# The recurrence of a hybrid transformer step: full-row tiles at two levels, moved transposes and increments, another mixer entry

## The chip, the cores and the metric

The kernel runs on one core of one Trainium2 chip. The metric is device time in microseconds (us). The kernel before was timed three times: median 2933.15 us, from 2932.75 to 2934.38. The engines are named as in the profile: PE is the matrix engine (PEld its weight loads), DVE the vector engine, ACT the scalar engine, POOL the general one, SP the queue that issues most DMAs.

## The reference, cut to what matters

One layer of a diffusion backbone on 1024 latent and 128 context tokens, width 1024: half a feed-forward block, a token mixer, the other half feed-forward block, each behind a normalisation with shift and scale. The mixer adds attention and a recurrence that runs forward and backward, and the recurrence is what the change is about.

```python
h = rmsnorm(x, g) * (1 + scale) + shift                  # the mixer's entry
q = silu(hq); v = hi; f = lb + (1 - lb) * sigmoid(hf)    # 8 heads of 64 keys, 64 values
# for each head and direction, token by token; k_t = 1 - f_t
S_t = diag(f_t) S_{t-1} + k_t outer v_t
o_t = S_t^T q_t
o_rec = rmsnorm(o_fw + flip(o_bw), hg_norm_g) * silu(hgate)
```

## The kernel before

Tokens lie along the free axis, 1152 columns (1024 latent, 128 context) in three chunks of 384. `ORDER` is (2, 0, 1), the order in which chunks are taken. Every large product is done in three single-pass parts of split numbers (`mm3`: high times high, high times low, low times high), which is why each weight and each activation exists as a high part (`wh`, `xh`) and a low part (`wl`, `xl`).

**The mixer's entry.** The first feed-forward block ends in `down_last`, which goes chunk by chunk and normalises a finished chunk (`norm`, lines 381 to 406) while the next is computed. The norm of the last chunk is left over as a generator, `self.tail`; the mixer advances it while it projects the other two chunks. `norm` first calls `stat_end`: one matmul `nps` with a matrix of ones sums the squares, then Ln and Exp on ACT and three DVE steps make the factor `rs`. For each of 8 row blocks it then multiplies on DVE, scales and shifts on ACT, rounds to `xh` on ACT and takes the rest `xl` on POOL.

**The recurrence** is `hgrn`. A head's forward direction lies in partitions 0 to 63 (`A`), its backward direction in 64 to 127 (`B`). For a chunk, `scan_pre` makes decayed keys `Kb`, `KE` and queries `Qb`, `QP` for blocks of 8 tokens. `scan_lev` then builds the token-by-token matrix `Af` by doubling: a base step (`Kb` with `Qb`, masked on DVE into the tiles `A`), then levels m = 8, 16, 32 and 64. At each level PE multiplies key copies `kr[m]` with `QP` into a PSUM tile `lv`; then DVE (rows B) and POOL (rows A) decay half of `QP`, which may start when the level's matmuls have read it and must end before the next level's; DVE decays `KE`, and ACT copies the next level's keys from it (`key_half`). `kr[m]` holds forward keys in the first half of each pair of blocks and backward keys in the second. At levels 8 and 16 one matmul over all 128 rows does both directions, with zeros in the other halves, and the result is masked. At levels 32 and 64 the directions are apart: rows A and rows B go to two `lv` tiles (lines 892 to 894), which ACT copies to `Af` (lines 913 and 914). There are three `lv` tiles (PSUM banks), taken in turn. After level 64, `kt` transposes `KE` through PE, ACT copies it to `kT`, and `dS` multiplies it with the values: the chunk's increment of the state. `scan_out` (after the third chunk) runs the state chain `S` on DVE and multiplies out (`po`).

**The order.** All of this is woven by generators: at each `yield` of `scan_lev` the loop in `hgrn` (lines 778 to 780) lets 12 large matmuls of a projection run (`mm`, half of one `dense_g` tile), and one step of the next chunk's `scan_pre`. So a chunk is: base, 12 mm, level 8, 12, level 16, 12, level 32, 12, level 64, 12, `kt`, 12, `dS`, 12. A scheduler then fixes each engine's order from this text; an engine runs its instructions in that order and waits where an operand is late. In every second head from the third on, the projections begin with `proj_gate`, which normalises the previous pair's output (`rec_norm`: matmuls `ops`, Ln and Exp with table loads on ACT, steps on DVE).

Of the kernel before, what the change touches and what calls it, by code (L numbers as in the profile page):

```python
# [19 lines left out]
P = 128  # L20
# [68 lines left out]
class Trunk:  # L89
# [3 lines left out]
    def run(self):  # L93
        self.part, self.mode, self.chunks, self.bg = {}, "ffn1", ORDER, iter(())
        nc, tc, a = self.nc, self.tc, self.a
        with ExitStack() as st:
            self.cp = st.enter_context(tc.tile_pool(name="cp", bufs=1))
            self.wp = st.enter_context(tc.tile_pool(name="wp", bufs=1))
            self.tp = st.enter_context(tc.tile_pool(name="tp", bufs=25))
            self.dp = st.enter_context(tc.tile_pool(name="dp", bufs=1, space=DRAM))  # L100
            self.consts()
            self.xs = self.dp.tile([KT, P, T], F32, name="xs")
            self.modt = self.cp.tile([P, 9, KT, 2], F32, name="modt")
            self.gs = self.cp.tile([P, 3, KT, 2], F32, name="gs")
            with ExitStack() as s1:
                self.ffn_pools(s1)
                self.start()
                self.ffn_fast(0, 2, 1)
            self.mode = "mix"
            with tc.tile_pool(name="mp", bufs=1) as mp:  # L110
                self.mixer_consts(mp)
                self.mixer()
            with ExitStack() as s1:
                self.mode = "ffn2"
                self.ffn_pools(s1)
                self.merge()
                self.ffn_fast(1, 8, 3)
# [263 lines left out]
    def norm(self, c, i):  # L381

        nc = self.nc
        lo, hi = span(c)
        cs = slice(lo, hi)
        rs = self.rs[:, cs]
        if self.mode != "mix":
            rs = self.bank("ps1", "rsp", hi - lo)
        self.stat_end(c, rs)
        yield  # L390
        for k in range(KT):
            t = self.fp.tile([P, hi - lo], F32, tag=self.nt[0], bufs=self.nt[1], name="xn")
            nc.vector.tensor_mul(t, self.x[k][:, cs], rs)
# [11 lines left out]
            nc.gpsimd.tensor_sub(tl, t, th)  # L405
            yield
# [204 lines left out]

    def mixer_consts(self, cp):
        nc, a = self.nc, self.a
# [5 lines left out]
        nc.vector.memset(self.onesb, 0.0)  # L619
# [34 lines left out]
    def proj_f(self, i, h, out):  # L654
        nc = self.nc
        fs = out["f"] = self.tt(F32, "fs")
        nc.vector.memset(fs[64:P, 0:1], 1.0)
        w = self.load_w(self.a["w_in"][i], KT, P, home="pieces" if i == 0 else "low")
        for c in ORDER:
# [16 lines left out]
    def proj_v(self, i, out):  # L676
        nc = self.nc
        V = out["V"] = self.tt(F32, "V")
        w = self.load_w(self.a["w_in"][i], KT, P, home="low")
        for c in ORDER:  # L680
# [34 lines left out]
    def hgrn(self):  # L715
        nc = self.nc
        self.mmb = 2
# [7 lines left out]
        self.A2 = f32("A2", [P, 3, G])  # L725
        for t in self.XY:
            nc.vector.memset(t[:, :, 3:4], 1.0)
        for t in self.A1 + [self.A2, self.kr[8], self.kr[16]]:
            nc.vector.memset(t, 0.0)
        self.cnt = 0  # L730
# [34 lines left out]

        d = scan_of(0)
        for _ in self.scan_pre(d, ORDER[0]):
            pass
# [72 lines left out]
    def scan_lev(self, d, b):  # L841
# [20 lines left out]
        def products(parts, k, q, blocks):  # L862
            for j in range(3):
                kj, qj = k[:, ts(j, P)], q[:, ts(j, P)]
                for ki, qi in blocks:
                    for r, ps in parts:
                        ks, qs = (ki, qi) if r != B else (qi, ki)
                        n = qs.stop - qs.start
                        nc.tensor.matmul(ps[ks, j, :n], kj[r, ks], qj[r, qs], start=True, stop=True)

# [15 lines left out]
        for li, m in enumerate((8, 16, 32, 64)):  # L886
            kr = self.kr[m]
            if m < G:
                ps = lv()
                products([(slice(0, P), ps)], kr, qp, diag)  # L890
            else:
                pair = (A, lv()), (B, lv())
                blocks = [(slice(u, u + m), slice(u + m, u + 2 * m)) for u in range(0, P, 2 * m)]
                products(pair, kr, qp, blocks)
            tv = Tm.rearrange("p (n h) -> p n h", h=2)
# [13 lines left out]
            if m < G:  # L909
                nc.vector.copy_predicated(A1, mb(2 + li), ps[:, :, :G])  # L910
            else:
                for u, v in blocks:
                    nc.scalar.copy(Af[u, :, v], pair[0][1][u, :, :m])
                    nc.scalar.copy(Af[v, :, u], pair[1][1][v, :, :m])
            if m == 16:
# [10 lines left out]
        nc.scalar.copy(kT, pt)  # L926
        yield
        pd = self.pp.tile([P, 3, 64], F32, tag="sm", bufs=3, name="dS")
# [4 lines left out]
        nc.scalar.copy(dS[:, 3 * b : 3 * b + 3], pd)  # L933
        yield

# [676 lines left out]
    def ffn_fast(self, l, gm, nxt):  # L1612
# [228 lines left out]
```

## Time and profile before

| What | us |
|---|---|
| median of 3 runs | 2933.15 |
| the profiled execution | 2932.25 |
| its span, first to last instruction | 2930.1 |
| feed-forward 1 with its end | to about 832 |
| recurrence with its projections | about 832 to 1472 |
| attention | to about 1914 |
| output, feed-forward 2, final norm | to the end |

The page of the profile gives for each engine the time in which it was busy. PE is busy nearly all the time everywhere, so what is to be read is the small rest: which instruction PE stood before, what released it, and at which clock PE ran. A row of the timeline reads: start, duration, engine, line, operation, output<-inputs, shape, count, and in brackets how long the engine was idle before it and what ended that. A view of stretches gives busy time of each engine between two times and the granted PE clock (1.00 is full). "mm" rows are the large projection matmuls; one with 384 columns starts about 0.175 us after the one before at full clock, 0.32 us at half.

### The profile page before, as it was taken

How to read it: one execution, taken by the hardware profiler on the slowest of the kernel's cores; microseconds unless marked ns; L12 is line 12 of the kernel's file. 1: busy time of each engine (PE TensorE's matmuls, PEld its weight loads, DVE VectorE, ACT ScalarE, POOL GpSimd, SP SyncE). 2: the span in 40 equal slices, each digit the busy share in tenths (PEclk: the TensorE clock that was granted, in tenths of full speed). 3: DMA queues.
4: the chain of work that ended last, by engine and by line, in shares of the span. 5: the costliest groups of instructions: out<-in, count | busy, mean ns of one | idle time of the engine just before them, and what ended most of it. 6: DMA issues, size and time to landing. Idle time of an engine off the chain costs nothing. (4 is left out here: it accounts for less than half of the span.)

```text
span 2930.1 us, 54396 instructions
## 1 busy us (share of the span) xinstructions
PE 2833.2 (97%) x20946; PEld 2668.0 (91%) x20946; DVE 1976.7 (67%) x4282; ACT 1285.9 (44%) x2574; POOL 957.3 (33%) x904
## 2 busy tenths in 40 slices
PE   6999999999999999999998999999999999999998
PEld 5999999999988888888996877699999999999997
DVE  7677777677678777777357777856665665556665
ACT  6432323321176666666536777721552332232112
POOL 0133322444132122222145444532342222235431
PEclk9999999999999999999998999999999999999999
DMA  6643333643111111111200001242542322235211
GB/s 245 206 146 122 122 127 111 255 162 119 61 61 66 40 55 42 55 42 53 73 31 14 16 18 34 74 163 72 165 147 93 108 83 75 75 120 199 92 46 65
DMA packets 151492, 282.44 MB, mean 96 GB/s; under 512 B 19201, under 2 KB 83777, under 8 KB 151233
## 3 DMA queue, kind: packets, MB, share of 16 engines
q1 hardware_dynamic: 151088, 278.90, 27.8%
q8 instruction: 165, 2.70, 0.4%
q14 instruction: 95, 0.77, 0.1%
q10 hardware_dynamic: 144, 0.07, 0.0%
HBM read 215.37 MB, written 63.52 MB: 95 GB/s over the span
## 5 line engine op out<-in xcount | busy, mean ns | idle before, releaser
L1590 PE MATMUL b<-xo,wo 128*128 128x288 f32 x3552 | 484.6, 296 | 0.0
L1590 PEld LDWEIGHTS b<-xo,wo 128*128 128x128 f32 x3552 | 476.4, 188 | 0.0
L483 DVE SCALAR_TENSOR_TENSOR x<-dn,modt,x 128x256 f32<-128x256 f32 (+4 forms) x728 | 353.3, 505 | 169.0 <-PE dn L456 168.1
L454 PE MATMUL mm<-xh,wh 128*128 128x384 f32 (+1 forms) x1008 | 363.5, 361 | 5.7 <-DVE q L673 3.7
L1590 PE MATMUL b<-bh,wo 128*128 128x288 f32 x1776 | 366.4, 295 | 0.6 <-ACT et L1600 0.6
L456 PE MATMUL mm<-xh,wl 128*128 128x384 f32 (+1 forms) x1008 | 342.8, 340 | 0.3 <-DVE wl L228 0.2
L455 PE MATMUL mm<-xl,wh 128*128 128x384 f32 (+1 forms) x1008 | 342.3, 340 | 0.0
L1590 PEld LDWEIGHTS b<-bh,wo 128*128 128x128 f32 x1776 | 289.2, 188 | 0.9 <-ACT et L1600 0.9
L1590 PE MATMUL b<-bl,wo 128*128 128x288 f32 x888 | 261.9, 295 | 0.0
L243 POOL TENSOR_TENSOR wl<-raw,wh 128x1024 fp32r<-128x1024 f32 (+3 forms) x71 | 152.0, 2142 | 267.8 <-ACT wh L242 265.0
L1565 ACT CAST wo<-raw 128x512 fp32r<-128x512 f32 x185 | 114.7, 621 | 229.5 <-PE b L1590 119.3
L454 PEld LDWEIGHTS mm<-xh,wh 128*128 128x128 f32 (+1 forms) x1008 | 189.8, 188 | 19.6 <-DVE q L673 4.3
L1566 DVE TENSOR_TENSOR wo<-raw,wo 128x512 fp32r<-128x512 f32 x185 | 127.1, 688 | 104.8 <-ACT wo L1565 101.9
L454 PE MATMUL dn<-hh,wh 128*128 128x384 f32 (+2 forms) x576 | 196.2, 341 | 1.3 <-DVE et L1606 0.8
L456 PE MATMUL dn<-hh,wl 128*128 128x384 f32 (+2 forms) x576 | 194.6, 338 | 1.0 <-POOL wl L243 1.0
L455 PE MATMUL dn<-hl,wh 128*128 128x384 f32 (+2 forms) x576 | 194.2, 337 | 0.0
L455 PEld LDWEIGHTS mm<-xl,wh 128*128 128x128 f32 (+1 forms) x1008 | 190.4, 189 | 1.9 <-issue 0.4
L456 PEld LDWEIGHTS mm<-xh,wl 128*128 128x128 f32 (+1 forms) x1008 | 189.9, 188 | 1.8 <-DVE wl L228 0.5
L1668 POOL TENSOR_TENSOR hl<-hr,hh 128x1152 fp32r<-128x1152 f32 x44 | 118.0, 2693 | 194.5 <-ACT hh L1667 100.7
L314 DVE SCALAR_TENSOR_TENSOR junk<-wada,cb 128x512 bf16<-128x512 f32 x224 | 165.0, 737 | 7.1 <-DMA wada<-in_w_aT 6.3
L1322 POOL TENSOR_TENSOR ehl<-e,ehl 128x512 fp32r<-128x512 f32 x93 | 122.6, 1323 | 141.7 <-ACT ehl L1320 78.8
L1590 PEld LDWEIGHTS b<-bl,wo 128*128 128x128 f32 x888 | 167.4, 189 | 0.0
(391 smaller groups left out, 6904.2 us busy)
## 6 DMA issues: line engine op xcount, KB each, us to landing
raw<-in_w SPq DMA_DIRECT2D x148, 256.0 KB, 3.2
raw<-in_w SPq DMA_DIRECT2D x58, 512.0 KB, 3.5
wada<-in_w_aT SPq DMA_DIRECT2D x112, 256.0 KB, 2.9
hr<-hs SPq DMA_DIRECT2D x44, 576.0 KB, 5.2
hs<-et SPq DMA_DIRECT2D x148, 144.0 KB, 1.7
raw<-in_w_in SPq DMA_DIRECT2D x41, 512.0 KB, 3.2
hb<-hd SPq DMA_DIRECT2D x44, 288.0 KB, 3.5
x<-in_xT SPq DMA_DIRECT2D x16, 576.0 KB, 6.4
```

The lines of the kernel that those rows point to most:

```text
L243: pin((eng or self.nc.gpsimd).tensor_sub(wl, raw, wh))
L314: nc.vector.scalar_tensor_tensor(junk, ws[n % 2], 1.0, cs[s], ALU.mult, ALU.mult, accum_out=o)
L454: pin(nc.tensor.matmul(ps, wh, xh, start=start and i == 0, stop=False))
L455: pin(nc.tensor.matmul(ps, wh, xl, start=False, stop=False))
L456: pin(nc.tensor.matmul(ps, wl, xh, start=False, stop=stop and i == n - 1))
L483: nc.vector.scalar_tensor_tensor(self.x[m][:, a:b], ps[:, a - lo : b - lo], self.modt[:, gm, m, s : s + 1], self.x[m][:, a:b], ALU.mult, A ...
L1322: eng.tensor_sub(el, e, eh)
L1565: nc.scalar.copy(wh, src[i])
L1566: nc.vector.tensor_sub(wl, src[i], wh)
L1590: nc.tensor.matmul(ps, w[:, k], x[:, k, :QW], start=first, stop=last, skip_group_check=home != i)
L1668: nc.gpsimd.tensor_sub(hl, raw, hh)
```

## The change

Seven edits, all around the mixer:

1. Levels 32 and 64 use one `lv` tile and matmuls over all 128 rows, as levels 8 and 16 do; the list of block pairs holds each pair in both orders. For this all four `kr` are cleared at the start, not two.
2. The copies to `Af` stand right behind the level's matmuls in the text, ahead of the decay.
3. The `yield` between level 64 and the transposes `kt` is gone; there is a second one behind level 8 and behind `kt`; the one behind `dS` is gone, so `dS` comes just ahead of the next chunk's base.
4. The last chunk's norm in the mixer: scale in the first DVE step, shift and rounding in one ACT step, the low part on DVE. Its `stat_end` has high priority.
5. The constants of the mixer (`mixer_consts`) are made and the mask is loaded during the first feed-forward block, the mask over SP's queue. The pool `mp` is gone.
6. The first chunk's `scan_pre` starts in the middle of the first projections, the clearing of the tiles is pinned behind the norm, and the weights of the projections `q` and `v` of the first pair are split in two pieces.
7. `tp` has 27 tiles of a full row block where it had 25; a scratch area for DMA descriptors is made smaller.

```diff
-            self.tp = st.enter_context(tc.tile_pool(name="tp", bufs=25))
+            self.tp = st.enter_context(tc.tile_pool(name="tp", bufs=27))
...
-            with tc.tile_pool(name="mp", bufs=1) as mp:
-                self.mixer_consts(mp)
-                self.mixer()
+            self.mixer()
...
+        last = self.mode == "mix"
+        if last:
+            with self.tc.high_priority(offset=600):
+                self.stat_end(c, rs)
+        else:
+            self.stat_end(c, rs)
...
+            if last:
+                for a, b, s in segs(c):
...
+                    nc.vector.scalar_tensor_tensor(v, self.x[k][:, a:b], g, rv, ALU.mult, ALU.mult)
+                    nc.scalar.activation(th, v, AF.Identity, bias=sh)
+                    nc.vector.scalar_tensor_tensor(tl, v, sh, th, ALU.add, ALU.subtract)
+                yield
+                continue
...
-        nc.scalar.dma_start(mf, a["mask"])
+        nc.sync.dma_start(mf, a["mask"])
...
-        w = self.load_w(self.a["w_in"][i], KT, P, home="low")
+        w = self.load_w(self.a["w_in"][i], KT, P, home="pieces" if i == 2 else "low")
...
-        for i, _ in enumerate(weave(feed(0))):
-            if i < 12:
-                next(self.tail, None)
-            if i == 11:
-                assert next(self.tail, 1)
...
-        d = scan_of(0)
-        for _ in self.scan_pre(d, ORDER[0]):
+        pre = iter(())
+        for i, _ in enumerate(weave(feed(0))):
+            if i < 12:
+                next(self.tail, None)
+            if i == 11:
+                assert next(self.tail, 1)
+                for t in self.XY:
+                    pin(nc.vector.memset(t[:, :, 3:4], 1.0))
+                d = scan_of(0)
+                pre = self.scan_pre(d, ORDER[0])
+            if i == 13:
+                for t in self.A1 + [self.A2] + list(self.kr.values()):
+                    pin(nc.vector.memset(t, 0.0))
+            next(pre, None)
+        for _ in pre:
             pass
...
-                        ks, qs = (ki, qi) if r != B else (qi, ki)
-                        n = qs.stop - qs.start
-                        nc.tensor.matmul(ps[ks, j, :n], kj[r, ks], qj[r, qs], start=True, stop=True)
+                        n = qi.stop - qi.start
+                        nc.tensor.matmul(ps[ki, j, :n], kj[r, ki], qj[r, qi], start=True, stop=True)
...
-            kr = self.kr[m]
-            if m < G:
-                ps = lv()
-                products([(slice(0, P), ps)], kr, qp, diag)
-            else:
-                pair = (A, lv()), (B, lv())
+            ps = lv()
+            blocks = diag
+            if m >= G:
                 blocks = [(slice(u, u + m), slice(u + m, u + 2 * m)) for u in range(0, P, 2 * m)]
-                products(pair, kr, qp, blocks)
+                blocks = [c for k, q in blocks for c in ((k, q), (q, k))]
+            products([(slice(0, P), ps)], self.kr[m], qp, blocks)
+            if m >= G:
+                for k, q in blocks:
+                    nc.scalar.copy(Af[k, :, q], ps[k, :, :m])
...
-            else:
-                for u, v in blocks:
-                    nc.scalar.copy(Af[u, :, v], pair[0][1][u, :, :m])
-                    nc.scalar.copy(Af[v, :, u], pair[1][1][v, :, :m])
...
             Tm = Tn
-            yield
+            if m < 64:
+                yield
+            if m == 8:
+                yield
...
         nc.scalar.copy(kT, pt)
+        yield
         yield
...
         nc.scalar.copy(dS[:, 3 * b : 3 * b + 3], pd)
-        yield
...
         if l == 0:
+            self.mixer_consts()
```

How the order moves, at three places. **PE, a chunk in the middle of a head** (`lv` are the recurrence's level matmuls, those with `Qb,Kb` the base; the rows left out are the projection matmuls `mm`, 12 in each gap of the first piece). Before:

```order
L869 MATMUL lv<-Qb,Kb 32x32 x24
...
L869 MATMUL lv<-QP,kr_9029 32x32 x12
...
L869 MATMUL lv<-QP,kr_9030 32x32 x12
...
L869 MATMUL lv<-QP,kr_9031 32x32 x12
...
L869 MATMUL lv<-QP,kr_9032 64x64 x6
...
L924 MATMUL kt<-ident,KE 128x128 x3
...
L932 MATMUL dS<-V,kT 64x64 x6
```

Now, with 12 rows of `mm` in each gap but 24 in the gap behind the first level and in the one behind `kt`:

```order
L949 MATMUL dS<-V,kT 64x64 x6
L885 MATMUL lv<-Qb,Kb 32x32 x24
...
L885 MATMUL lv<-QP,kr_9026 32x32 x12
...
L885 MATMUL lv<-QP,kr_9027 32x32 x12
...
L885 MATMUL lv<-QP,kr_9028 32x32 x12
...
L885 MATMUL lv<-QP,kr_9029 64x64 x6
L940 MATMUL kt<-ident,KE 128x128 x3
```

Levels 16, 32 and 64 come 12 `mm` later after the base, `kt` follows level 64 at once, and `dS` stands 24 `mm` behind `kt` and directly ahead of the next base.

**DVE, first chunk of a head that begins with `proj_gate`** (`rt`, `osq` and `oT` are the steps of `rec_norm`, `QP` the decay of the queries: 64x12x16 between levels 16 and 32, 64x6x32 between 32 and 64). Before:

```order
L905 TENSOR_TENSOR QP<-QP,T_11346 64x12x16
L910 COPY_PREDICATED A_0_9035<-mask,lv 128x96
L917 TENSOR_TENSOR Ad<-A_0_9035,A_9037 128x96
L363 SCALAR_TENSOR_TENSOR rt<-ops,osq 128x384 x2
L364 SCALAR_TENSOR_TENSOR rt<-rt,osq 128x384 x2
L365 SCALAR_TENSOR_TENSOR osq<-rt,osq 128x384 x2
L968 SCALAR_TENSOR_TENSOR oT<-oT,vec,osq 128x384 x2
L363 SCALAR_TENSOR_TENSOR rt<-ops,osq 128x384
L905 TENSOR_TENSOR QP<-QP,T_11421 64x6x32
```

Now:

```order
L361 SCALAR_TENSOR_TENSOR rt<-ops,osq 128x384 x2
L362 SCALAR_TENSOR_TENSOR rt<-rt,osq 128x384 x2
L363 SCALAR_TENSOR_TENSOR osq<-rt,osq 128x384 x2
L984 SCALAR_TENSOR_TENSOR oT<-oT,vec,osq 128x384 x2
L361 SCALAR_TENSOR_TENSOR rt<-ops,osq 128x384
L922 TENSOR_TENSOR QP<-QP,T_11327 64x12x16
L362 SCALAR_TENSOR_TENSOR rt<-rt,osq 128x384
L927 COPY_PREDICATED A_0_9032<-mask,lv 128x96
L363 SCALAR_TENSOR_TENSOR osq<-rt,osq 128x384
L930 TENSOR_TENSOR Ad<-A_0_9032,A_9034 128x96
L984 SCALAR_TENSOR_TENSOR oT<-oT,vec,osq 128x384
L715 TENSOR_TENSOR sg<-mm,sg 128x384
```

The decay that level 32 needs stood ahead of `rec_norm` and now stands behind nine of its twelve steps; the one that level 64 needs (64x6x32) is now the row after the last one shown.

**PE, the mixer's entry** (`dn` is the end of the feed-forward block, `nps` the sum of squares for the last chunk). Before, `nps` stands behind the first 12 `mm`:

```order
L456 MATMUL dn<-hh,wl 128x384
L454 MATMUL mm<-xh_8434,wh 128x384
...
L456 MATMUL mm<-xh_8440,wl 128x384
L438 MATMUL nps<-rs,ones 128x384
L454 MATMUL mm<-xh_8434,wh 128x384
```

Now it stands ahead of them:

```order
L467 MATMUL dn<-hh,wh 128x384
L468 MATMUL dn<-hl,wh 128x384
L469 MATMUL dn<-hh,wl 128x384
L451 MATMUL nps<-rs,ones 128x384
L467 MATMUL mm<-xh_8446,wh 128x384
```

What had filled PE while the squares were summed up now comes after the sum.

More of the change, by code (lines that the diff above doesn't have):

```diff
@@ L392, in norm @@
             t = self.fp.tile([P, hi - lo], F32, tag=self.nt[0], bufs=self.nt[1], name="xn")
+            if last:
+                for a, b, s in segs(c):
+                    v, th, tl = t[:, a - lo : b - lo], self.xh[k][:, a:b], self.xl[k][:, a:b]
+                    g, sh = self.gs[:, i, k, s : s + 1], self.modt[:, 3 * i, k, s : s + 1]
+                    rv = rs[:, a - lo : b - lo]
+                    nc.vector.scalar_tensor_tensor(v, self.x[k][:, a:b], g, rv, ALU.mult, ALU.mult)
[3 more added lines that the diff above has]
+                continue
             nc.vector.tensor_mul(t, self.x[k][:, cs], rs)
@@ L657, in proj_f @@
         nc.vector.memset(fs[64:P, 0:1], 1.0)
-        w = self.load_w(self.a["w_in"][i], KT, P, home="pieces" if i == 0 else "low")
+        w = self.load_w(self.a["w_in"][i], KT, P, home="pieces" if h == 0 else "low")
         for c in ORDER:
@@ L678, in proj_v @@
         V = out["V"] = self.tt(F32, "V")
-        w = self.load_w(self.a["w_in"][i], KT, P, home="low")
+        w = self.load_w(self.a["w_in"][i], KT, P, home="pieces" if i == 3 else "low")
         for c in ORDER:
@@ L715, in hgrn @@
     def hgrn(self):
-        nc = self.nc
+        nc, pin = self.nc, self.tc.keep_in_program_order
         self.mmb = 2
@@ L725, in hgrn @@
         self.A2 = f32("A2", [P, 3, G])
[L726 to L729, printed above, removed]
         self.cnt = 0
@@ L1819 @@
     from concourse.bass_utils import run_bass_kernel_spmd
-    nc = _bacc.Bacc("TRN2", target_bir_lowering=False, num_devices=1)
+    nc = _bacc.Bacc("TRN2", target_bir_lowering=False, num_devices=1, dynamic_dma_scratch_size=1024)
     arrays = layout(inputs)
```

5 lines of the change are left out of this document (2 added, 3 removed).

## The prediction

> **What bounds the kernel now.** I read the page first, then a table of stretches of the recurrence, then the waits of PE there, then the timeline at the longest of them.
>
> ```profile
> span 2930.1 us, 54396 instructions
> PE 2833.2 (97%) x20946; PEld 2668.0 (91%) x20946; DVE 1976.7 (67%) x4282; ACT 1285.9 (44%) x2574; POOL 957.3 (33%) x904
> ```
>
> PE is busy for 97% of the span, so a change can win only what PE stands, or runs slowly, in the stage that is changed. The stretches show the recurrence (1028 to 1172 is one period of two heads) and four windows of 3.4 us:
>
> ```profile
> core 0: us, PE busy (x) PEld busy (x) DVE busy (x) ACT busy (x) POOL busy (x), PEclk, DMA share, GB/s
> 832.00:905.00 73.00, 63.60 (x459) 58.13 (x459) 56.38 (x133) 56.15 (x118) 25.99 (x33) 0.95 0.15 51
> 1028.00:1172.00 144.00, 138.01 (x1544) 122.34 (x1543) 108.51 (x276) 96.06 (x225) 31.45 (x52) 0.99 0.14 48
> 1037.10:1040.50 3.40, 1.82 (x14) 1.44 (x13) 2.56 (x6) 3.25 (x11) 1.54 (x2) 1.00 0.16 60
> 1040.50:1043.90 3.40, 3.40 (x14) 3.30 (x13) 2.18 (x4) 2.46 (x5) 1.25 (x1) 0.50 0.00 0
> 1078.10:1081.50 3.40, 1.93 (x20) 1.52 (x18) 2.47 (x10) 3.25 (x12) 0.00 (x0) 1.00 0.02 5
> 1081.50:1084.90 3.40, 3.40 (x22) 3.33 (x21) 2.21 (x4) 3.26 (x9) 1.64 (x4) 1.00 0.07 28
> ```
>
> A period loses 6.0 us to standing. The mixer's entry loses 9.4 of 73. The fourth row is a second loss: after a window in which PE was busy for 1.82 of 3.40 us, the next one ran at clock 0.50. The window at 1078.10 was hardly busier (1.93), and the next one kept clock 1.00. Who holds PE up, from 905 to 1456 us:
>
> ```profile
> PE lv L869 <- ACT Af L913: 10.3, 9, 1.6
> PE dS L932 <- ACT kT L926: 3.1, 3, 1.0
> PE lv L869 <- ACT kr L882: 2.4, 3, 0.8
> PE lv L869 <- DVE QP L905: 1.8, 5, 0.7
> ```
>
> The first row is the bank wait: level 64 takes two `lv` tiles of three and stands until ACT has copied level 32 out of one. The second is `dS`, only 12 `mm` behind the transposes.
>
> **The change part by part.** *One tile per level.* A chunk takes six `lv` tiles instead of eight; level 64 then gets the bank of level 8, which DVE has read long before. Of the nine bank waits three, of 1.58 us, are where a head begins with `proj_gate`; the other six make 10.3 - 3 x 1.58 = 5.6 us. All of it can go, or none if another operand is as late; I take 5.
>
> The three places with `proj_gate` are worked out alone, since the order changes there:
>
> ```profile
> 1037.10 0.53 ACT L362 ACTIVATE osq<-osq 128x384 f32<-128x384 f32 x1
> 1037.35 0.33 PE L454 MATMUL mm<-xh,wh 128*128 128x384 f32 x1
> 1037.66 0.56 DVE L363 SCALAR_TENSOR_TENSOR rt<-ops,osq 128x384 f32<-128x384 f32 x1 [0.34 <-ACT osq L362]
> 1038.25 0.61 DVE L905 TENSOR_TENSOR QP<-QP,T 64x192 f32<-64x192 f32 x1
> 1039.25 0.56 PE L869 MATMUL lv<-QP,kr 64*64 64x64 f32 x6 [1.58 <-ACT Af L913]
> 1040.57 0.52 PE L456 MATMUL mm<-xh,wl 128*128 128x384 f32 x1
> ```
>
> Before, PE reached 1037.35 with levels 16 and 32 done and stood until 1039.25, then ran a window at half clock: 10 or 11 `mm` at 0.32 instead of 0.175 us, 1.5 us lost. Now DVE decays `QP` for level 32 only behind the third `rt`. That step waits for the Exp that ended at 1037.6; the decay would end near 1038.5. PE, with 36 `mm` before it as before, would want level 32 at about 1037.2: a new wait of 1.3 us. Level 64 comes 11 `mm` later (1.9 us), while DVE still has six steps of about 0.5 us ahead of its decay: another 0.5. Per place 1.58 + 1.5 - 1.8 = 1.3, three times 3.9. If PE stands as long as before and the clock drops again, it is -2; if neither wait comes, 9.
>
> What the full rows cost PE stands in one chunk:
>
> ```profile
> 887.85 0.40 PE L869 MATMUL lv<-QP,kr 128*32 128x32 f32 x24
> 893.08 0.39 PE L869 MATMUL lv<-QP,kr 64*32 64x32 f32 x24
> 896.89 0.63 PE L869 MATMUL lv<-QP,kr 64*64 64x64 f32 x12 [1.12 <-POOL QP L905]
> 902.60 0.57 PE L932 MATMUL dS<-V,kT 128*64 128x64 f32 x12 [0.35 <-ACT kT L926]
> ```
>
> The same 24 records take 0.40 us on full rows (level 8) and 0.39 on half rows (level 32); 12 records with 64 columns take 0.57 (`dS`, which also waited before it) and 0.63. I take 0. A full-row matmul must also wait for both halves of `QP`; that is inside the waits above.
>
> *Twice the distance.* `dS` gets 24 `mm` (4.2 us) behind `kt` instead of 2.1; its longest wait is 1.0. The waits go: 3.1 us, and 0.35 in the row just shown: 3.5, between 0 and that. Level 16 gets the same; the rows charge it with 0.65 once, left in the range.
>
> *`dS` joined to the base.* Each change from `mm` to a small group and back costs PE:
>
> ```profile
> 901.91 0.34 PE L456 MATMUL mm<-xh,wl 128*128 128x384 f32 x1
> 903.10 0.44 PE L454 MATMUL mm<-xh,wh 128*128 128x384 f32 x1
> 905.13 0.34 PE L456 MATMUL mm<-xh,wl 128*128 128x384 f32 x1
> 905.40 0.62 PE L869 MATMUL lv<-Qb,Kb 64*32 64x32 f32 x48
> 905.95 0.44 PE L454 MATMUL mm<-xh,wh 128*128 128x384 f32 x1
> 906.23 0.33 PE L455 MATMUL mm<-xl,wh 128*128 128x384 f32 x1
> ```
>
> From 905.13 to 906.23 are 1.10 us, two `mm` steps would be 0.35: the base costs 0.75, of which 0.10 is the entry (0.27 to its start instead of 0.175) and 0.10 the slower first `mm` behind it (0.28); `dS` hands over in about 0.1 more. One such crossing less is about 0.3 us, in two chunks of three of 8 heads: 16 x 0.3 = 4.8, at least 0 and at most 16 x 0.55, the whole of one entry and one exit. Level 64 with `kt` behind it saves nothing sure, since `kt` had no gap before; `KE` for `kt` is decayed one chunk ahead in DVE's order, so I add no wait.
>
> *The state chain.* At a head's end `dS` now lies 12 `mm` nearer to `po`:
>
> ```profile
> 1086.28 0.57 PE L932 MATMUL dS<-V,kT 128*64 128x64 f32 x12
> 1090.04 2.78 DVE L943 SCALAR_TENSOR_TENSOR S<-S,Gall,dS 64x64 f32<-64x64 f32 x9
> 1091.18 0.44 PE L953 MATMUL po<-Af,V 128*64 128x128 f32 x4
> ```
>
> With `dS` 2.1 us later, at 1088.4, a copy on ACT ends it before 1090.04, when DVE comes to the chain anyway; and `po` needs only its first three steps (0.9 us) at once. Cost 0. Without that cover it is up to 1 us at each of 8 heads.
>
> *The entry.*
>
> ```profile
> 836.81 0.91 PE L438 MATMUL nps<-rs,ones 128*128 128x384 f32 x2 [1.59 <-DVE rs L379]
> 842.13 0.17 DVE L619 MEMSET onesb<- 128x128 f32 x1 [2.03 <-POOL xl L405]
> 844.71 0.54 DVE L363 SCALAR_TENSOR_TENSOR rt<-nps,rs 128x384 f32<-128x384 f32 x1
> 853.16 0.69 PE L454 MATMUL mm<-xh,wh 128*128 128x384 f32 x1 [2.48 <-DVE q L673]
> ```
>
> DVE's steps up to `rs` are the same, so `nps` still starts near 836.8, and the 12 `mm` that ran before it are put behind it: 2.1 us lost, PE stands 4.4 instead of 1.59. In return the clearing of the constants (842.13 to 844) and the wait for POOL ahead of it leave DVE, and `rt` can start some 2 us sooner. ACT loses one step for each of 8 blocks, POOL one, DVE gains one of 0.54 us: 4.3 us more work on DVE. Against the 2.48 us at 853.16 I set a like wait, as the first sigmoid now stands on ACT behind three new rounding steps. I take 0, between -6 (the 4.3 and 2.1 uncovered) and +5 (the wait at 853.16 and the 2.1 us by which the norm comes sooner, with that loss hidden). The mask's load, 27 tiles, the earlier constants and the split weights cost nothing where PE does not wait for them; the two pieces cost ACT one more start each.
>
> The waits for `kr` and the other `QP` (4.5 us) I leave as they are. **Sum:** 5 + 3.9 + 3.5 + 4.8 = 17.2 from the profiled execution's 2932.25 (its span and 2.15 around it): 2915.0; the median of the runs is 0.9 above it: 2916, rounded to **2915** for the small gains left out. By its terms' bounds the likeliest case reaches from 2905 to 2925.
>
> **The clock, by the skill.** The row said that 1.58 us of standing were enough for a window at 0.50. The Trainium skill, "TensorE: Matmul & The Clock Gate", section "Why this matters for your kernels", asks only for no gap over some 3 us. By that rule the 1.5 us per `proj_gate` place would not be there to win (the sum would be 4.5 us smaller) and the 4.4 us at the entry would cost a window. The trace contradicts it for the first; the second it cannot show.
>
> **The rivals.** (a) *The wait moves on.* ACT, not the bank, is late: in the window at 1037.10 it is busy for 3.25 of 3.40 us. Then PE meets the same lateness at the next ACT result (`kr`, the sigmoid that frees an `mm` tile), and only the joining stays: 2933.15 - 4.8 = 2928. For it: the waits on `kr` in the list. Against: next to ACT's 96.06 of 144 us over a period there is room, and what level 64 waited for is truly a bank.
>
> (b) *Slower: the two halves ran side by side.* If matmuls on rows A and on rows B overlap, full rows take twice as long at levels 32 and 64: 24 chunks x (0.39 + 0.63) = 24.5 us lost, 2915 + 24.5 = 2940. It decides once a pair of levels takes over 0.7 us more than before. Against it stands the pair 0.40 and 0.39.
> The Trainium skill, "TensorEngine Tiling (Array Packing)", section "Theoretical Speedup", gives up to 2x for a dimension up to 64 by such tiles, which speaks against this change; the trace does not agree, by that pair.
>
> (c) *All waits go* and nothing returns, at the gates and at `kr`: 2915 - 5 - 4.5 = 2905.
>
> **How the numbers follow.** Forecast 0.64, (a) 0.17, (b) 0.08, (c) 0.11. What can be told from no change is 0.2%, 5.9 us, so below 2927.3 is faster: forecast, (c), and a third of (a), 0.80; the rest of (a) with little else, 0.12; (b) 0.08. The range, 2904 to 2931, holds the forecast, (a) and half of (c).
>
> **What would show it.** Right: no wait of `lv` on `Af`, none of `dS` on `kT`; `nps` behind an idle time over 4 us; at the three gates level 32 waits about 1 us for DVE's `QP` and no window at 0.50 follows; level groups of 24 records still near 0.4 us. Wrong: a new long row of PE waits on `QP`, `kr` or `KE`, more windows at half clock, or level 32 at 0.8 us.

## The result and the profile after

| | us |
|---|---|
| kernel before, median of 20 runs | 2932.61 (2929.70 to 2935.93) |
| changed kernel, median of 20 runs | 2926.81 (2922.73 to 2931.57) |
| ratio | 0.998, 95% interval 0.9973 to 0.9987 |
| profiled execution of the changed kernel, its span | 2924.97, 2923.2 |

The change gains 5.8 us, about a third of the 18 forecast. The first lines of the page and a table of stretches of the changed kernel (the mixer's entry, one period of two heads), to be set beside those of before:

```profile
span 2923.2 us, 54347 instructions
PE 2820.2 (96%) x20946; PEld 2663.8 (91%) x20946; DVE 1981.7 (68%) x4292; ACT 1284.4 (44%) x2568; POOL 947.7 (32%) x896
```

```profile
833.99:905.00 71.01, 62.84 (x446) 58.88 (x446) 56.00 (x132) 50.64 (x108) 17.75 (x25) 0.93 0.15 51
1030.60:1172.70 142.10, 135.29 (x1542) 121.60 (x1542) 108.26 (x275) 96.44 (x225) 30.73 (x51) 0.99 0.14 49
```

PE executes the same 20946 matmuls. A period has fallen from 143.8 us (between the first `ops` rows of two `proj_gate`) to 142.1, yet PE still stands 6.8 us in it (142.10 - 135.29), where it stood 6.0 before. So the standing did not go; it changed its cause. PE's waits from 828 to 1500 us (what PE waited for, us in total, times, longest), in the changed kernel:

```profile
PE lv L885 <- DVE QP L922: 21.1, 24, 3.0
PE nps L451 <- DVE rs L377: 4.5, 1, 4.5
PE mm L467 <- DVE q L686: 2.6, 1, 2.6
PE vt L699 <- ACT t L696: 2.4, 7, 0.5
PE lv L885 <- POOL QP L922: 1.4, 1, 1.4
```

The rows of `lv` on `Af`, of `dS` on `kT` and of `lv` on `kr` have disappeared, 10.3, 3.4 and 2.4 us over this stretch before. In their place stands a single row of 21.1 us, which was 1.8: the level products wait for DVE to decay `QP`. With POOL's row it is 22.5 us (2.9 before). This is the "new long row of PE waits on QP" which the prediction named as the sign that it is wrong.

Where the longest of these waits comes from is seen in the timeline of the third chunk of an even head. First before the change: DVE's decay of `QP` for level 16, two of its rows between, its decay for level 32, and PE's level 16 and level 32.

```profile
1072.83 0.35 DVE L905 TENSOR_TENSOR QP<-QP,T 64x192 f32<-64x192 f32 x1
...
1073.39 0.71 DVE L905 TENSOR_TENSOR KE<-KE,T 64x192 f32<-64x192 f32 x2
1073.65 0.40 PE L869 MATMUL lv<-QP,kr 128*32 128x32 f32 x24
1074.02 0.55 DVE L823 TENSOR_TENSOR Kb<-kk,Y 64x384 f32<-64x384 f32 x1
...
1076.25 0.35 DVE L905 TENSOR_TENSOR QP<-QP,T 64x192 f32<-64x192 f32 x1
1076.28 0.75 PE L869 MATMUL lv<-QP,kr 64*32 64x32 f32 x24
```

Then the same place in the changed kernel:

```profile
1072.29 0.35 DVE L922 TENSOR_TENSOR QP<-QP,T 64x192 f32<-64x192 f32 x1
...
1073.67 0.40 PE L885 MATMUL lv<-QP,kr 128*32 128x32 f32 x24
...
1073.96 0.55 DVE L840 TENSOR_TENSOR Kb<-kk,X 64x384 f32<-64x384 f32 x1
...
1077.25 1.38 DVE L923 TENSOR_TENSOR T<-T 128x24 f32<-128x24 f32 x3
...
1078.85 0.36 DVE L922 TENSOR_TENSOR QP<-QP,T 64x192 f32<-64x192 f32 x1
...
1079.35 0.40 PE L885 MATMUL lv<-QP,kr 128*32 128x32 f32 x24 [2.97 <-DVE QP L922]
```

Between the two decays lay 3.4 us before (1072.83 to 1076.25) and lie 6.6 us now. DVE now does the four products `Kb` and `Qb`, the factors `TK` and `TQ` and four steps of `T` of the *next* chunk there. PE does not come earlier than before: level 16 starts at 1073.67 (1073.65 before), and behind the same 12 `mm` PE wants level 32 some 2.7 us later (2.6 before). It is the decay that comes 2.6 us later, and PE stands 2.97 us. Over all 24 chunks, worked out from the rows of the two timelines, DVE is busy for 2.2 us on average between these two decays before and for 4.3 us now, while PE reaches level 32 2.6 and 2.7 us (median) behind the start of level 16, its waits left out. Of the 22.5 us PE waits 1.4 at level 16, 16.7 at level 32 and 4.4 at level 64.

What the wait does to the clock (stretches of the 3.41 us in which the granted clock changes):

```profile
1076.53:1079.94 3.41, 0.59 (x25) 0.58 (x26) 3.14 (x11) 2.34 (x7) 2.16 (x4) 1.00 0.01 2
1079.94:1083.35 3.41, 3.41 (x12) 3.24 (x11) 3.31 (x8) 3.30 (x10) 1.04 (x3) 0.50 0.00 0
1216.47:1219.88 3.41, 2.00 (x12) 1.67 (x10) 3.26 (x10) 2.06 (x4) 0.67 (x1) 1.00 0.01 2
1219.88:1223.29 3.41, 1.78 (x32) 1.77 (x33) 3.18 (x11) 2.27 (x10) 2.61 (x6) 1.00 0.00 0
```

The wait at 1076 falls into one such stretch and the next runs at clock 0.50, which costs another 1.7 us (half of 3.41). The same wait in the next period is cut in two by the border at 1219.88, and no half clock follows.

### The profile page after: what moved, and what is told of

It is laid out like the page before. It is cut to its first block, busy times and chain, and to the rows that moved or that the text cites. A ratio compares the mean times of both kernels' runs of the same rounds, so it can differ in the third digit from the quotient of the medians.

```text
span 2923.2 us, 54347 instructions
## 1 busy us (share of the span) xinstructions
PE 2820.2 (96%) x20946; PEld 2663.8 (91%) x20946; DVE 1981.7 (68%) x4292; ACT 1284.4 (44%) x2568; POOL 947.7 (32%) x896
```

## The experiments

The runs ask four things: which edit brings the wait, whether DVE's order or its load is behind it, what the place of the `mm` does, and what the entry costs. The ratios are to the kernel before, run on the same chip; differences to the changed kernel's 2926.81 compare chips, on which the medians of the kernel before lie between 2932.61 and 2933.59. The waits on `QP` (DVE's row and POOL's) are those from 828 to 1500 us, 22.5 us in the changed kernel; some expectations call them 24, with gaps counted that the list of waits leaves out.

| Run | median us | ratio, 95% interval | waits on `QP` |
|---|---|---|---|
| changed kernel | 2926.81 | 0.9980 (0.9973 to 0.9987) | 22.5 |
| e1 no extra step behind level 8 | 2963.93 | 1.0108 (1.0094 to 1.0121) | 27.8 |
| e2 step behind 16 instead | 2928.54 | 0.9986 (0.9977 to 0.9995) | 26.1 |
| e3 half rows | 2934.10 | 1.0008 (0.9999 to 1.0017) | 13.6, and `Af` 7.0 |
| e4 recurrence alone | 2931.46 | 0.9995 (0.9987 to 1.0004) | 22.7 |
| e5 decays first, all chunks | 2938.53 | 1.0023 (1.0013 to 1.0032) | 16.3 |
| e6 casts on POOL | 2938.83 | 1.0026 (1.0017 to 1.0036) | 27.1 |
| e7 both | 2969.46 | 1.0132 (1.0116 to 1.0147) | 19.8 |
| e8 entry alone | 2929.93 | 0.9992 (0.9983 to 1.0001) | 2.3 |
| e9 steps behind 8 and 16 | 2926.75 | 0.9980 (0.9971 to 0.9989) | 18.3 |
| e10 steps behind 8, 16, 32 | 2916.61 | 0.9941 (0.9928 to 0.9953) | 9.5 |
| e11 no rests | 2922.54 | 0.9967 (0.9955 to 0.9980) | 19.0 |
| e12 `dS` apart | 2924.39 | 0.9967 (0.9954 to 0.9979) | 20.9 |
| e13 decays first, three chunks | 2927.03 | 0.9981 (0.9973 to 0.9990) | 20.7 |
| e14 `nps` behind the `mm` | 2926.94 | 0.9980 (0.9971 to 0.9989) | 22.4 |
| e15 e10 and e14 | 2917.73 | 0.9946 (0.9933 to 0.9958) | 9.3 |
| e16 before, with steps 8, 16, 32 | 2928.32 | 0.9988 (0.9979 to 0.9997) | 2.9 |

### Which edit brings the wait (e1 to e4, e8)

e1 takes the second `yield` behind level 8 out again; `V` is then looked up when a head begins.

```diff
-            if m == 8:
-                yield
```

> The changed kernel without the extra step of other work behind level 8 (12 mm instead of 24 ahead of level 16; all else as changed). Theories: Q (the queue): with the extra step DVE's order holds 16 to 18 instructions of the next chunk between the QP decays for level 16 and for level 32 in the worst chunks, 186 in the 24 chunks together against 100 before; here 104. Then PE's 22.5 us of waits of lv on QP fall under 8, the half-clock windows at 1080 and 1363 go, and the time is 2915, 2911 to 2920. H (full rows wait for both halves of QP, the halves do not): the waits stay above 16 us, time 2924 to 2930. E (the entry ate the gain): waits on QP fall but the time stays above 2922.

e2 moves it:

```diff
-            if m == 8:
+            if m == 16:
                 yield
```

> The extra step of 12 mm is moved from behind level 8 to behind level 16, so that PE has 24 mm ahead of level 32. DVE's order has 83 instructions between the two decays over the 24 chunks. Q: level 32 no longer waits (its 17.9 us over 24 chunks fall under 3), what is left is level 64, up to 5.5, and level 16, up to 1.5; time 2912, 2907 to 2917. H: PE still waits for the later half but has 2.1 us more, so it would gain too: this run alone does not tell Q from H, the next does. E: above 2920.

e3 takes levels 32 and 64 back to pairs of half-row tiles and leaves the steps:

```diff
-            ps = lv()
+            two = (A, lv()), (B, lv())
...
-            products([(slice(0, P), ps)], self.kr[m], qp, blocks)
+            products(two, kr, qp, blocks)
```

> The changed kernel with levels 32 and 64 back in pairs of half-row tiles as before (two lv tiles, two products per block), the new steps kept. DVE's order between the decays is that of the changed kernel (186). Q: PE still waits for the decays, now on QP's half B or inside the group, and the bank waits on Af come back in addition: 2926 to 2936. H: the QP waits fall under 6 us and only the Af waits (up to 10) come back: 2914 to 2922.

e4 puts the changed `scan_lev`, with all four `kr` cleared, into the kernel before:

```diff
-        for t in self.A1 + [self.A2, self.kr[8], self.kr[16]]:
+        for t in self.A1 + [self.A2] + list(self.kr.values()):
```

> The kernel before with the changed level code alone (full rows, one tile, new steps, dS joined); the mixer's entry, the constants, the pieces are those of before. DVE has 181 instructions between the decays. Q: the recurrence alone gives what the whole change gave, 2927, 2924 to 2930, and its QP waits are again about 20 us. E: the recurrence alone gives the forecast 2915 to 2919 and the entry had cost the rest (8 to 12 us).

e8 is its opposite, the changed kernel with the `scan_lev` of before:

> The changed kernel with the level code of before (pairs of half-row tiles, old steps): only the new entry, constants and pieces remain. By the run with the recurrence alone (2931.5, 1.2 under before) the entry must carry the other 4.6 of the 5.8 us: 2928, 2925 to 2931. If the two parts only pay together: 2931 to 2934.

The waits, first of e1, then of e2, then of e3:

```profile
PE lv L886 <- DVE QP L923: 27.3, 24, 2.2
PE po L971 <- DVE S L958: 13.3, 6, 3.1
```

```profile
PE lv L885 <- DVE QP L922: 24.9, 21, 3.7
```

```profile
PE lv L886 <- DVE QP L922: 7.1, 9, 1.2
PE lv L886 <- ACT Af L930: 7.0, 11, 1.5
PE lv L886 <- POOL QP L922: 6.5, 4, 2.2
```

e1 and e2 missed. Without the step the waits did not fall, though DVE works for only 2.3 us between the decays for 16 and 32. They stand mostly at levels 16 and 32 (13.3 and 9.0 us), the state chain `S` comes too late for `po`, and the kernel is slower than before. e1 does not isolate the step's effect on DVE's order, though: it also leaves a chunk 72 `mm` instead of 84. With the step behind 16 level 32 no longer waits, but levels 16 and 64 do. The wait follows the places where only 12 `mm` lie between two levels. e3 speaks against the theory that full rows cause it: with half rows the waits on `QP` stay at 13.6 us, where that theory had under 6, the bank wait returns, the waits of `lv` sum to 20.6 us (7.1 + 7.0 + 6.5), and the kernel loses 7.3 us against the changed one. e4 and e8 split the gain: the recurrence, for which 17.2 us were forecast, gives 1.2 by itself, its interval reaching across no change (outside both ranges expected of e4); the entry, forecast at nothing, gives some 3 (its interval just includes no change). The whole change gives 5.8, more than the two together. In e4's profile PE runs 23.9 us of the recurrence at half clock, in the changed kernel's 10.2, which makes some 7 us; what the recurrence alone is worth hangs on that.

### Order or load of DVE (e5 to e7, e11, e13)

e5 queues each step of the next chunk's preparation on DVE behind the `QP` decay written last. That is issue order alone, without a wait:

```diff
                     next(work, None)
-                    next(pre, None)
+                    with self.tc.issue_after(self.dec):
+                        next(pre, None)
...
```

> The changed kernel; on DVE each step of the next chunk's preparation is queued behind the last QP decay that was written ahead of it (issue order only, no wait added). In the worst chunk 4 to 6 instructions instead of 18 stand between the decays for level 16 and for level 32. Theories, after the first four runs, in which the wait moved to another level instead of going: O (order): it is only what stands ahead of the decay in DVE's queue; then PE's waits of lv on QP fall from 24 us under 8, and the time is 2912, 2907 to 2918. D (DVE is full while a head's three chunks run, some 16 of 18.7 us per chunk, and any order leaves something late): the waits stay above 15 us or come back on Kb, KE or kr, time 2921 to 2930.

e6 has POOL compute the rests in the mixer:

```diff
-                self.nc.vector.tensor_sub(wl[:, k], raw[:, k], wh[:, k])
+                (self.nc.gpsimd if self.mode == "mix" else self.nc.vector).tensor_sub(wl[:, k], raw[:, k], wh[:, k])
```

> The changed kernel; the rounding rests wl of the mixer's weights (60 instructions of 0.69 us on DVE, 40 us in the recurrence) are made by POOL, which is busy for 145 of 546 us there. D: 1.7 us per chunk leave DVE, the waits on QP fall from 24 to 12 us or less, time 2917, 2911 to 2921. O: 15 instructions still stand ahead of the decay in the worst chunks, those three waits stay near 2 to 3 us, time 2922 to 2927; later than that if POOL's own QP decays now wait behind the casts.

e7 joins the two edits:

> Both edits of the two runs before. O: the same as the run with the decays first, within 2 us. D: better than each alone, 2908 to 2914.

e5's waits:

```profile
PE lv L886 <- DVE QP L923: 16.3, 17, 1.9
PE vt L699 <- ACT t L696: 10.1, 6, 3.2
PE po L974 <- DVE S L961: 5.6, 8, 1.0
```

In the third chunks the wait at level 32 did go, as "order" said. But other chunks waited up to 1.9 us for `QP`, and what had been pushed back on DVE came late for `vt` and `po`, so the sum grew. e5, e6 and e7 all came out above both their ranges. e6 can't decide on the load, since the casts came back as a cost on DVE itself (DVE is busy for 399.56 us from 905 to 1451 us, 388.33 in the changed kernel), and e7, slowest of all, has the cost of both. The timeline of e6 beside a cast on POOL:

```profile
1106.64 3.18 POOL L233 TENSOR_TENSOR wl<-raw,wh 128x512 fp32r<-128x512 f32 x2 [14.16 <-ACT wh L230]
1107.05 1.64 DVE L841 TENSOR_TENSOR Qb<-qx,Y 64x384 f32<-64x384 f32 x1
1108.70 1.55 DVE L840 TENSOR_TENSOR Kb<-kk,Y 64x384 f32<-64x384 f32 x1
1110.17 0.55 DVE L841 TENSOR_TENSOR Qb<-qx,X 64x384 f32<-64x384 f32 x1
```

The same product takes 0.55 us alone and 1.55 to 1.64 beside the cast. So e11 takes the load off DVE without giving it to POOL: it leaves out the rests, and the third product of a step uses the rounded weight.

```diff
...
             self.nc.scalar.copy(wh, raw)
-            for v in range(2):
-                k = slice(4 * v, 4 * v + 4)
-                self.nc.vector.tensor_sub(wl[:, k], raw[:, k], wh[:, k])
-            return wh, wl
+            return wh, wh
```

> The changed kernel without the rounding rests of most mixer weights: the third product of each step uses the rounded weight itself (the part of the result that the rests give is left out); PE runs the same matmuls, DVE 60 instructions of 0.69 us less (1.7 us per chunk), nothing is added on POOL. D: waits on QP fall from 24 under 12 us, time 2916, 2911 to 2921. O: 15 instructions stand between the decays in the worst chunks; the three waits of 3 us at level 32 stay above 2 us, the sum above 17, time 2923 to 2927.

e13 applies e5's order in three chunks only:

```diff
+                    if n == 2 and h in (2, 4, 6):
+                        with self.tc.issue_after(self.dec):
+                            next(pre, None)
+                    else:
+                        next(pre, None)
...
```

> The changed kernel; only in the third chunk of the heads 2, 4 and 6, where level 32 waited for 3 us, the preparation is queued on DVE behind the QP decay written ahead of it (5 instead of 18 instructions between the two decays; order only). O (the wait is set by the DVE work that stands between two decays against the mm between two levels): these three waits go (9 us) and the half-clock windows behind two of them (3 us), the rest stays: waits on QP near 14 us, time 2916, 2912 to 2920. If lateness only moves on (to level 64, to po, to vt) as it did when all chunks were ordered: 2922 to 2930.

e11's row of waits, then those of e13:

```profile
PE lv L882 <- DVE QP L919: 19.0, 20, 3.2
```

```profile
PE lv L889 <- DVE QP L926: 19.3, 22, 1.8
PE po L977 <- DVE S L964: 4.7, 3, 1.6
```

Both theories were too simple. With 40 us less work on DVE the waits fell by 3.5 us only, the 3 us wait stayed (3.2), and the time fell by 4.3, between the two ranges and with intervals that just overlap; so the load of the whole stage is at most a part of it, and not the larger one. With the order mended where it was worst, the three long waits and the half-clock stretches behind them disappeared, but `po` now waited 1.6 us for the state chain three times and level 32 of the next chunk 1.60 us, and the time stayed (2927.03). So the order decides *where* PE waits; mending it there did not make up the time. What DVE is short of shows in two stretches, from the base of a head's second chunk to level 64 of its third and from there to the next head's base: first in the changed kernel, then, in the third row, the former stretch in the kernel before.

```profile
1047.34:1084.00 36.66, 33.55 (x427) 30.57 (x423) 32.98 (x84) 26.05 (x67) 10.52 (x19) 0.95 0.16 53
1084.00:1098.39 14.39, 14.39 (x113) 12.95 (x109) 7.57 (x25) 4.87 (x14) 0.50 (x1) 1.00 0.19 68
1047.61:1084.50 36.89, 33.88 (x430) 30.30 (x430) 31.13 (x79) 25.98 (x67) 11.22 (x20) 1.00 0.14 46
```

DVE is busy for 90% of the first (32.98 of 36.66; 84% before, 31.13 of 36.89) and 53% of the second, in which PE runs `mm` in one block and never stands. PE's spare work lies where DVE doesn't need the time.

### Where the mm lie (e9, e10, e12, e16)

These move `mm` out of that block to between the levels. e9 doubles the step behind 8 and 16 (`if m < G`, where `G` is 32), e10 behind 8, 16 and 32:

```diff
-            if m == 8:
+            if m < 64:
                 yield
```

> The changed kernel with a further step of 12 mm behind level 16 (24 mm ahead of levels 16 and 32). The mm come out of the block that PE runs at a head's end, so PE gets no more work. From level 8 of one chunk to level 8 of the next were 20.6 us before and 18.7 in the changed kernel; here 20.8. D (DVE has some 16 us of work per chunk, waits come from the shorter distance): waits on QP fall from 24 under 10 us, time 2915, 2910 to 2920. O (order alone): DVE's worst chunk has 12 instructions between the decays for 16 and 32, level 64 is not helped: waits move to level 64 as in the run with the step behind 16 alone, above 18 us, time 2925 to 2930.

> The changed kernel with further steps of 12 mm behind level 16 and behind level 32 (24 mm ahead of levels 16, 32 and 64): 22.9 us from chunk to chunk. D: waits on QP under 4 us. The head's end then has only some 2 us of mm left, and the products po and the state chain S lose cover: up to 1 us at each of 8 heads. Time 2914, 2909 to 2922. O: DVE holds 215 instructions between the two decays, more than in the changed kernel (186), so the waits stay above 15 us: 2924 to 2930.

e12 adds the `yield` behind `dS` again:

> The changed kernel with dS no longer joined to the next base: a step of 12 mm stands between them, as before. D: 20.8 us from chunk to chunk, DVE is relieved as in the run with two further steps: waits on QP under 12 us; the crossings cost 4.8 us again (16 x 0.3): 2920, 2915 to 2925. O: DVE holds 135 instructions between the two decays, 8 in the worst chunk instead of 18: the waits fall as well, so this run does not tell D from O, but prices the joining: if the time is above 2927, the join pays more than the waits cost; if below 2922, the join was what cost the forecast its 12 us.

e16 is the kernel before with e10's steps alone:

> The kernel before with a further step of 12 mm behind levels 8, 16 and 32 and nothing else. If the steps alone carry the gain (more mm between two levels hide both the bank waits and the decays), 2920, 2916 to 2924, with the Af waits gone. If the gain of three steps needs one tile per level and the join, 2928 to 2934.

The waits of e9, then of e10, then of e16:

```profile
PE lv L885 <- DVE QP L922: 16.4, 16, 2.5
PE po L972 <- DVE S L959: 5.5, 16, 1.7
```

```profile
PE lv L885 <- DVE QP L922: 9.5, 7, 1.6
PE dS L949 <- ACT kT L942: 4.8, 7, 0.8
```

```profile
PE mm L454 <- DVE sg L702: 6.6, 4, 1.9
PE mm L454 <- DVE q L673: 6.3, 2, 4.0
...
PE lv L869 <- POOL QP L905: 2.4, 8, 0.4
...
PE lv L869 <- ACT Af L913: 1.5, 4, 0.5
PE lv L869 <- DVE QP L905: 0.5, 2, 0.3
```

With 24 `mm` ahead of each of the three levels the waits on `QP` fall to 9.5 us, no half-clock stretch is left between 905 us and the end of the recurrence, and a period takes 138.3 us, from the `ops` at 1029.6 to those at 1167.9. With e15, which differs from it only at the entry, that is the best kernel of the study: 16 us under before and 10 under the change. In its timeline DVE does *more* between the decays for 16 and 32 than in the changed kernel (251 instructions against 226 over all chunks, 4.9 us on average against 4.3), so that alone is not what counts, against what the theory of the order expected: it now stands against 24 `mm`, 4.35 us, where it stood against 12. It is the place of the `mm` and not their number in a chunk: e12 gives a chunk 12 more as well, not between the levels, and keeps 20.9 us of waits on `QP`. e9 fell short: its waits went to level 64, as that theory had said, and its time did not improve. e12 shows no gain from the join: without it the median is 2.4 us lower, but the two intervals overlap, and a chunk has 12 `mm` more, so it does not price the join alone. In the kernel before the same steps remove the bank waits too (10.3 to 1.5), but its `mm` then wait for `sg` and `q`; they gain 0.12%. e10's 0.59% need the change's edits as well as its own; which of them, no run tells.

### The entry (e14, e15)

```diff
-            with self.tc.high_priority(offset=600):
-                self.stat_end(c, rs)
+            self.stat_end(c, rs)
```

> The changed kernel without the raised priority at the entry: nps stands behind the 12 mm again, the only move on PE. The changed kernel stands 4.5 us for it and then runs at half clock for 6.8 us. If this stall is lost time: 2 to 5 us faster, 2923, 2921 to 2925. If the norm then comes later by as much as PE is busy longer (the first mm wait for it): no difference, 2925 to 2929.

> The steps behind levels 8, 16 and 32 (2916.6 in the run before) together with the entry of the run above: 2913, 2911 to 2915, if that stall is lost time; 2916 to 2918 if not.

The waits of e14 at the entry:

```profile
PE mm L466 <- ACT sg L663: 3.8, 1, 3.8
...
PE nps L450 <- DVE rs L377: 1.6, 1, 1.6
```

The 4.5 us for `nps` become 1.6, and the first `mm` that need a sigmoid's bank wait 3.8 instead of 0.3. The sum of PE's waits and the time are the same: the stall was free. From the last `dn` row to the first level product PE takes 49.0 us here and 48.1 with the raised priority. e15 agrees, at 2917.73 against e10's 2916.61.

## Why the prediction was wrong

**The step that failed** is the sentence "The waits for `kr` and the other `QP` (4.5 us) I leave as they are", and with it "A full-row matmul must also wait for both halves of `QP`; that is inside the waits above". The waits on `kr` went, but those on `QP` grew by 19.6 us (2.9 to 22.5). Of these 4.5 are the gates' (3 x (1.22 + 0.28)), which the sum had counted; 15.1 were not in it, nor two half-clock stretches behind them (3.4 us). The prediction followed DVE's order at the three gates only, "since the order changes there". It changes in every head: with a second step of `mm` behind level 8, DVE's order puts more of the next chunk's preparation ahead of the decay that level 32 needs. Between the decays for levels 16 and 32 DVE now works for 4.3 us instead of 2.2; the doubled `mm` stand one level earlier, ahead of level 16, so that 4.3 us meet 12 `mm` of 2.2 us, and 16.7 of the 22.5 us are waits at level 32 (3 x 1.22 of them the gates'). e2 repeats it one level on: with the second step behind level 16, DVE works for 1.8 us between these two decays and for 4.8 between those for 32 and 64, and 17.1 of its 26.1 us are waits at level 64.

Rival (a), "the wait moves on", came nearer with its 2928 than the forecast, but for another reason than the one it gives: it has ACT late. At most the 4.4 us at level 64, where the bank wait used to stand, are a wait that moved on, and there to DVE.

The rows show the late decay, and e10 that more `mm` at these places win. Half rows do not bring the waits under 6 us (e3), and mending the order in three chunks only moves the wait on (e13). Two things stay open. In e1, without a second step, DVE works for only 2.3 us between either pair of decays, and yet PE waits, mostly at level 16; a chunk is shorter there by 12 `mm`. And how much of the wait is DVE's order and how much its load, no run separates.

**Bank waits, 5 us: right** for the row, which is gone. What the row did not show is that a wait inside a group costs more than its idle time. Before the change level 64 was often interrupted behind its second record:

```profile
1079.26 0.33 PE L869 MATMUL lv<-QP,kr 64*64 64x64 f32 x2
1081.05 0.56 PE L869 MATMUL lv<-QP,kr 64*64 64x64 f32 x10 [1.47 <-ACT Af L913]
```

From the start of the last `mm` ahead of such a group to that of the second behind it, less two `mm` steps and the idle time, it cost PE 0.98 to 1.02 us, and 0.69 where nothing interrupted it: 0.3 us more in each of 11 chunks. e3 prices the pair of half-row tiles at 7.3 us with the new steps, and not by standing: PE stands 26.0 us there from the first level product to the last `mm`, 27.9 in the changed kernel, but runs 20.5 us of it at half clock instead of 10.2.

**The gates, 3.9 us: right.** The place that stood 1.58 us, in the changed kernel:

```profile
1040.28 0.35 DVE L922 TENSOR_TENSOR QP<-QP,T 64x192 f32<-64x192 f32 x1
...
1040.78 0.40 PE L885 MATMUL lv<-QP,kr 128*32 128x32 f32 x24 [1.22 <-DVE QP L922]
...
1043.87 0.57 PE L885 MATMUL lv<-QP,kr 128*64 128x64 f32 x12 [0.28 <-DVE QP L922]
```

1.22 and 0.28 were forecast as 1.3 and 0.5, and no half-clock stretch follows: 4.7 us for the three.

**Full rows cost nothing: right,** 0.40 and 0.57 us a group in the same rows, where rival (b) needed over 0.7 us more for the pair.

**Twice the distance: right** for `dS` (3.4 to 0), but the second step went ahead of level 16, which had waited only 0.65 us once, and not ahead of levels 32 and 64, where e10 shows that it was wanted.

**The join, 4.8 us: too large.** In the rows of `dS` and base the entry saved is 0.1 us (0.27 instead of 0.175 to the group's start) and the slower first `mm` 0.1; the handing over of `dS` costs the same either way. 16 x 0.2 = 3.2 us.

**The state chain, 0: right** in the changed kernel (no row of `po` on `S`), and close to its edge: the row stands in e1, e5, e7, e9 and e13, and smaller in e10, e15 and e16.

**The entry, 0: inside its bounds.** From the last `dn` row to the first level product are 50.2 us before and 48.1 now, 2.1 us won; e8's median, less sharp, gives some 3. `nps` does stand 4.5 us, and e14 confirms that this costs nothing in the end. The Trainium skill, "TensorE: Matmul & The Clock Gate", section "Why this matters for your kernels", would have such a gap followed by a slow stretch; here it was, 6.8 us at clock 0.50. Before the change the entry had 6.8 us at 0.50 as well, in two pieces.

**The sum** with these sizes: 17.2 - 15.1 - 3.4 + 2.4 (`kr`) - 1.6 (the join) + 2.1 (the entry) = 1.6 us against 5.8 measured. What is missing shows in the stretch from the first level product to the last `mm`, 661.4 us before and 657.2 now in the profiled executions. PE stood in it for 22.6 us before and for 27.9 now, and had 10.2 us at half clock both times: before at the three gates, now behind two waits on `QP` and, at 885 us, behind the 2.6 us for `q`. So the removed waits won nothing on balance: what was won is 9.5 us of PE's own time (661.4 - 22.6 against 657.2 - 27.9). Of these 3.2 are the join, 3.3 the 11 interrupted groups, and 2.0 the three gates, where level 64 stood in two pieces of 0.68 and 0.75 us and is now one of 0.77; 1 us is left open. The prediction began with "a change can win only what PE stands, or runs slowly"; the time from group to group, which the profile counts as busy and of which it priced only the join, was where this one won.

## What to carry to other kernels

A removed wait is a gain only if the next operand of the same chain is in time. Before counting it, go on to that operand and set the in-order work of its producer, from one step to the next (here 4.3 us on DVE), against the work that the busy engine has between those steps (12 `mm`, 2.2 us). A moved step can change the order of every engine, so look at all of them and not only where a change is expected. Where the busy engine has too little between two steps, look for filler work which runs in one block elsewhere and move it there; reordering the late engine's queue only chose who waits. And price the passage between large and small groups, which counts as busy: here it was what the recurrence won.

## What the runs showed of the hardware

Work handed from DVE to POOL slowed DVE: a 64x384 product took 1.55 to 1.64 us beside POOL's cast and 0.55 alone, and the cast itself, 0.69 us on DVE, took 1.44 on POOL (mean of 60). The kernel lost 12 us against the changed one (e6). The Trainium skill, "Perfetto Trace Analysis", section "Optimizing Scalar/DVE Operations", says that the two share a read port and that moving work between them may not help. The trace agrees that it did not help; the port itself no run here shows.

A wait of 3 us cost half clock or not by how it lay to the 3.41 us stretches: with 0.59 us of PE work in one stretch the next ran at 0.50, with 2.00 and 1.78 us in two neighbours both went on at 1.00. Before the change 1.82 of 3.40 us had been followed by 0.50, so the busy share alone does not tell.
